# Two-layer hybrid backbone: large products as one float32 matmul in place of three float32r matmuls on high and low parts, and the MLP's tiles taken in groups of four

## The chip, the cores and the metric

The kernel runs on one core of a Trainium2 chip. The metric is the device time of one execution in microseconds, the median of several runs; lower is better. One profiled execution gives the trace from which all rows below are taken. The engines are named as the profile names them: PE (matrix multiplication; PEld is its weight load), DVE (vector), ACT (scalar, activations), POOL (general purpose) and SP, whose queue issues all DMAs of this kernel.

## The reference

Two layers over 1024 latent tokens and 256 context tokens of width 1024, everything in float32:

```
for i in range(DEPTH):                      # DEPTH = 2
    h  = modulate(x,  norm1_g, sh1, sc1)    # adaLN: rmsnorm(x, g) * (1 + scale) + shift
    (q, k, v), feat = project_tokens(h, w_in, ...)   # ONE input projection, 1024 -> 2480 columns
    attn = mla_attend(q, k, v)              # 8 heads, q/k of 96, v of 64; softmax over 1280 keys
    gdn  = gdn_mix(feat, ...)               # bidirectional gated delta rule, 4 heads of 128
    x = x + g1 * (concat([attn, gdn]) @ w_out)
    x = x + g2 * (square(relu(modulate(x, norm2_g, sh2, sc2) @ w_ff1)) @ w_ff2)   # D_FF = 4096
return rmsnorm(x, final_norm_g)
```

The context tokens go through the same weights, attend only to themselves, and are dropped after attention in the last layer. The modulation vectors are `silu(c) @ w_ada + b_ada`.

## The kernel before

Features lie with the 1024 channels on partitions, in 8 tiles (`KD` = 8), and the tokens along the free side in three blocks (`BLOCKS`): 256 context tokens, then twice 512 latent tokens. A product with a [128, 1024] weight tile is therefore 8 matmuls of 128 x 128 weights over 256 or 512 columns that accumulate in one bank of PSUM. Each layer has three stages.

Stage 1 (`stage1`): the norm, the input projection (`product`, 20 weight tiles of output columns), a short convolution on DVE (`conv_tile`, L442 to L450), the low-rank key, value and query projections (`kv_proj`, `q_proj`), and the chunk preparation of the delta rule (`Prep.decay`, with the product `dps` at L1421).

Stage 2 (`stage2`): attention in units of 256 queries of one head, 40 units in layer 0 and 32 in layer 1, and between them the steps of the delta rule (`delta`, its products are `g`). A unit has a `front` (scores `S` and `St`, their maximum, the exponential, the reciprocal of the sums) and a `back` (transposes `pt`, then the product with the values, `o`, at L916). The front of one unit is interleaved with the back of the unit before (`PATTERN`). The reciprocals go through DRAM (`rinv`, L902, then `rb`, L904) so that they lie along the queries; `ob` is the unit's result times `rb`.

Stage 3 (`stage3`): the output projection (`out_tile`, `ops`), the second norm, and the MLP: `ff1` makes one tile of 128 hidden columns for one block (`fps`, then relu and square), `ff2` multiplies a group of `FB` such tiles by the second weight (`f2ps`) and DVE adds the result to `x` at L1304. In layer 0, DVE also computes the modulation of later norms by multiply-and-sum in this stage (`ada_tile`, L272).

All large products are made in float32r: each operand is kept as a float32r high part and the remainder as a low part, and `mm3` issues high x high, high x low and low x high into the same bank. `wload` loads a weight tile and makes its parts: ACT copies the high part (L307), POOL subtracts to get the low part (L308). `norm_mod`, `lowrank`, `parts`, `ff1` and stage 3's load of `cat` do the same for the features. For attention, the low part of the values lies beside the high part in one 128-column weight, and the probabilities are split on the way out of PSUM: ACT makes `ph` (L927), DVE makes `pl` (L928). The small products of the delta rule, the transposes and the first modulation (`row`, L199) are plain float32 already.

Python code issues the instructions in program order; a scheduler of the tile framework then orders them on each engine by its own estimate of time. Each engine, and SP's queue of DMAs, runs its list in order.

Of the kernel before, what the change touches and what calls it, by code (L numbers as in the profile page):

```python
# [8 lines left out]
F32 = mybir.dt.float32  # L9
F32R = mybir.dt.float32r  # L10
BF16 = mybir.dt.bfloat16
AF = mybir.ActivationFunctionType
ALU = mybir.AluOpType
# [4 lines left out]
P = 128  # L18
# [16 lines left out]
W_BUFS = 3  # L35
# [38 lines left out]
def host_layout(inp):  # L74
# [16 lines left out]
    # tiles of output columns: q 4, k 4, v 4, misc, kv_a, q_a 2, z 4  # L91
# [4 lines left out]
    # the rotary columns: first halves of all heads, second halves of all heads  # L96
# [19 lines left out]
class K:  # L116
# [13 lines left out]
    # ---------------------------------------------------------------- set-up  # L130
# [35 lines left out]
    def start(self, mmp, pjp, tpp, stp):  # L166
        """Modulation of the first norm, the first norm, and the first two output tiles, as the features come."""
        nc, io, cst = self.nc, self.io, self.cst
        with ExitStack() as es:
# [12 lines left out]
            # features and weights are queued behind the modulation's weights  # L182
# [64 lines left out]
            for d in range(2):  # L247
                t = cst.tile([P, P], F32R, name=f"mlr{d}")
# [27 lines left out]
    def ada_sum(self, l, v, m):  # L276
        """Eight columns that came by way of Pool and ACT, from their halves and the bias."""
# [4 lines left out]
    def load_sc(self, sp):  # L282
        """silu(c) and silu(c_ctx) on all partitions."""
# [6 lines left out]
    def gain(self, l, j, vs):  # L290
        """(1 + scale) * gain of norm j."""
# [19 lines left out]
    def mm3(self, ps, lh, ll, rh, rl, start, stop, then=lambda i: None):  # L311
        mm = self.nc.tensor.matmul
        then(mm(ps, lhsT=lh, rhs=rh, start=start, stop=False))  # L313
        then(mm(ps, lhsT=lh, rhs=rl, start=False, stop=False))  # L314
        then(mm(ps, lhsT=ll, rhs=rh, start=False, stop=stop))  # L315
# [21 lines left out]
    def norm_mod(self, xs, rb, b, l, which, pool):  # L337
        """Modulated RMSNorm of block b (8 tiles [128, n]) into the high and low parts of h."""
# [478 lines left out]
    def attention(self, l, last, ap, psA, psO):  # L817
# [4 lines left out]
        def parts(hi, lo, src):  # L822
# [669 lines left out]
```

## Time and profile before

| | |
|---|---|
| time, median of 3 runs | 3947.9 us (3941.03 to 3948.28) |
| span of the profiled execution, first to last instruction | 3929.9 us |
| what lies around the span (median less span) | 18.0 us |
| PE busy | 3517.4 us (90%), 19001 matmul records |
| DVE, ACT, POOL busy | 2134.2 us (54%), 1459.3 us (37%), 1516.0 us (39%) |
| mean granted clock of PE | 0.937 of full speed |
| DMA | 372.52 MB, mean 95 GB/s |

"Busy" is the time during which at least one instruction of the engine is under way. Successive matmuls overlap in the array, so the duration of a single record is longer than the distance from its start to the next one's start; for a stream it is the distance that counts. "x12" in a row of the timeline means twelve records that follow one another. The granted clock is 1.00 at 2.4 GHz and 0.50 at 1.2 GHz; values between are averages over a stretch.

### The profile page before, as it was taken

The numbers are of one execution on the slowest core, as the hardware profiler recorded it, in microseconds if no ns is written. First come the engines' busy times: TensorE is split into PE (matmuls) and PEld (weight loads), VectorE is DVE, ScalarE is ACT, GpSimd is POOL, SyncE is SP. The second block draws the span as 40 slices with busy tenths as digits, with TensorE's granted clock in tenths as the row PEclk, the third lists the DMA queues.
The fourth block names the chain that finished last, engine by engine and source line by source line (L and its number), as shares of the span: only waits on it lengthen the run. The fifth ranks groups of instructions, "written<-read, shape, count | busy, mean of one in ns | idle before, by whom it ended". The sixth has DMA issues, their size and how long they took to land.

```text
span 3929.9 us, 52618 instructions
## 1 busy us (share of the span) xinstructions
PE 3517.4 (90%) x19001; PEld 2992.1 (76%) x19001; DVE 2134.2 (54%) x4080; ACT 1459.3 (37%) x3156; POOL 1516.0 (39%) x1358
## 2 busy tenths in 40 slices
PE   8789977887887898999999978888889899999998
PEld 4668766787776777888888757767788788888887
DVE  5157855565769995333333627776667533333334
ACT  4334355565633111121112524336666531222122
POOL 3124864433354232232223313675533352333232
PEclk8899987898998899999999979989899899999999
DMA  5343465535353352111111334454653511111111
GB/s 186 91 136 116 139 149 94 112 93 95 77 199 102 129 180 81 43 44 38 38 33 43 102 94 132 144 147 109 125 101 81 132 57 46 52 51 49 44 54 54
DMA packets 335892, 372.52 MB, mean 95 GB/s; under 512 B 126849, under 2 KB 226577, under 8 KB 333969
## 3 DMA queue, kind: packets, MB, share of 16 engines
q1 hardware_dynamic: 335632, 369.18, 34.3%
q8 instruction: 149, 2.44, 0.3%
q14 instruction: 111, 0.90, 0.1%
HBM read 280.65 MB, written 88.42 MB: 94 GB/s over the span
## 4 chain that ended last, share of the span: by engine, by line
PE 57%; DVE 13%; DMA 12%; issue 5%; ACT 4%; POOL 3%; SPq 1%; POOLq 0%; DVEq 0%; ACTq 0%
PE f2ps L313 6%; PE f2ps L314 6%; PE f2ps L315 6%; PE fps L314 6%; PE fps L315 6%; PE fps L313 6%; DVE adaj L272 3%; DMA raw<-kd 3%; PE g L984 3%; PE o L916 3%; PE pt L924 2%; DVE cacc L444 2%; DVE A L1427 2%; DMA rinv<-rinv 2%; DMA adaw<-w_adaT 1%
## 5 line engine op out<-in xcount | busy, mean ns | idle before, releaser
L308 POOL TENSOR_TENSOR wlo<-wraw,whi 128x1024 fp32r<-128x1024 f32 (+1 forms) x190 | 462.3, 2441 | 1217.8 <-ACT whi L307 1217.8
L1304 DVE SCALAR_TENSOR_TENSOR x<-f2ps,mod,x 128x512 f32<-128x512 f32 (+1 forms) x648 | 440.9, 689 | 353.3 <-PE f2ps L315 353.1
L307 ACT CAST whi<-wraw 128x1024 fp32r<-128x1024 f32 (+1 forms) x190 | 195.6, 1046 | 1008.0 <-PE f2ps L314 692.7
L313 PE MATMUL f2ps<-ah,whi 128*128 128x512 f32 (+1 forms) x1296 | 474.4, 371 | 31.4 <-DVE x L1304 27.2
L314 PE MATMUL f2ps<-al,whi 128*128 128x512 f32 (+1 forms) x1296 | 478.5, 370 | 0.8 <-DVE al L1293 0.8
L313 PE MATMUL fps<-hh,whi 128*128 128x512 f32 (+1 forms) x1288 | 471.3, 368 | 8.8 <-ACT hh L351 8.8
L315 PE MATMUL f2ps<-ah,wlo 128*128 128x512 f32 (+1 forms) x1296 | 477.4, 369 | 0.0
L314 PE MATMUL fps<-hl,whi 128*128 128x512 f32 (+1 forms) x1288 | 474.1, 368 | 0.0
L315 PE MATMUL fps<-hh,wlo 128*128 128x512 f32 (+1 forms) x1288 | 472.9, 368 | 0.0
L1293 DVE TENSOR_TENSOR al<-relu,ah 128x256 fp32r<-128x256 f32 (+1 forms) x161 | 111.5, 699 | 512.9 <-POOL relu L1292 512.9
L313 PE MATMUL mm<-hh,whi 128*128 128x512 f32 (+1 forms) x880 | 333.1, 380 | 35.0 <-ACT craw L430 22.1
L314 PE MATMUL mm<-hl,whi 128*128 128x512 f32 (+1 forms) x880 | 331.4, 377 | 3.6 <-DVE hl L352 2.1
L315 PE MATMUL mm<-hh,wlo 128*128 128x512 f32 (+1 forms) x880 | 327.6, 374 | 0.8 <-POOL wlo L308 0.8
L928 DVE TENSOR_TENSOR pl<-pt,ph 128x512 fp32r<-128x512 f32 x328 | 222.2, 686 | 194.7 <-ACT ph L927 182.1
L313 PEld LDWEIGHTS f2ps<-ah,whi 128*128 128x128 f32 x1296 | 248.2, 192 | 74.4 <-DVE x L1304 29.9
L313 PEld LDWEIGHTS fps<-hh,whi 128*128 128x128 f32 x1288 | 243.7, 190 | 49.1 <-ACT hh L351 9.1
L314 PEld LDWEIGHTS f2ps<-al,whi 128*128 128x128 f32 x1296 | 248.7, 192 | 40.7 <-DVE al L1293 1.0
L315 PEld LDWEIGHTS f2ps<-ah,wlo 128*128 128x128 f32 x1296 | 248.4, 192 | 40.1
L314 PEld LDWEIGHTS fps<-hl,whi 128*128 128x128 f32 x1288 | 244.0, 189 | 40.1 <-POOL hl L357 0.3
L315 PEld LDWEIGHTS fps<-hh,wlo 128*128 128x128 f32 x1288 | 243.9, 189 | 39.8
L924 PE MATMUL pt<-ctab,p 128*128 128x128 f32 x1312 | 219.9, 287 | 32.9 <-ACT p L896 12.7
L1292 POOL TENSOR_TENSOR relu<-relu 128x256 f32<-128x256 f32 (+1 forms) x161 | 159.5, 996 | 225.2 <-ACT ah L1291 209.7
(287 smaller groups left out, 7520.6 us busy)
## 6 DMA issues: line engine op xcount, KB each, us to landing
wraw<-w_ff SPq DMA_DIRECT2D x128, 512.0 KB
adaw<-w_adaT SPq DMA_DIRECT2D x160, 256.0 KB
wraw<-w_in SPq DMA_DIRECT2D x40, 512.0 KB
QK<-QK SPq DMA_DIRECT2D x72, 256.0 KB
A<-A SPq DMA_DIRECT2D x40, 256.0 KB
v<-vtd SPq DMA_DIRECT2D x40, 256.0 KB
kt<-ktd SPq DMA_DIRECT2D x40, 256.0 KB
kT<-kTd SPq DMA_DIRECT2D x36, 256.0 KB
```

What stands on the lines that cost most here:

```text
L272: nc.vector.tensor_tensor_reduce(out=j, in0=w, in1=self.sc_b[v][:, s], op0=ALU.mult, op1=ALU.add, scale=1.0, scalar=acc if i else self.bad ...
L307: nc.scalar.copy(hi[:, :n], raw[:, :n])
L308: nc.gpsimd.tensor_tensor(lo[:, :n], raw[:, :n], hi[:, :n].bitcast(F32), op=ALU.subtract)
L313: then(mm(ps, lhsT=lh, rhs=rh, start=start, stop=False))
L314: then(mm(ps, lhsT=lh, rhs=rl, start=False, stop=False))
L315: then(mm(ps, lhsT=ll, rhs=rh, start=False, stop=stop))
L916: nc.tensor.matmul(o, lhsT=v[:, k, :], rhs=x[:, j, :], start=k == 0 and i == 0, stop=k == nkt - 1 and i == 1)
L924: self.mark = nc.tensor.transpose(tp[:, j, i * P:(i + 1) * P], pp[i][:, (k0 + j) * P:(k0 + j + 1) * P], self.ident)
L928: nc.vector.tensor_tensor(pl, tp, ph.bitcast(F32), op=ALU.subtract)
L984: nc.tensor.matmul(ps[:, h, :], lhsT=lhs[:, h, :], rhs=rhs[:, h, :], start=True, stop=True)
L1292: nc.gpsimd.tensor_tensor(r[:, :n], r[:, :n], r[:, :n], op=ALU.mult)
L1304: nc.vector.scalar_tensor_tensor(xs, ps[:, :n], g2, xs, op0=ALU.mult, op1=ALU.add)
```

## The change

The high and low parts go away. Weights, features, keys, queries, values and probabilities are kept as float32, and each product is a single float32 matmul. With the parts go the instructions that made them: the ACT copies and POOL or DVE subtractions in `wload`, `norm_mod`, `lowrank`, `parts`, `Prep.decay`, `ff1` and the load of `cat`. The probabilities leave PSUM in one copy, alternately by ACT and DVE. The values are a 64-column weight, so the unit's result needs no addition of two halves, and DVE multiplies it by `rb` straight out of PSUM (before: ACT copied a half, DVE added, POOL multiplied). The squared relu is made by POOL alone. The memory that this frees goes into 10 weight tiles in flight (3 before), into 4 tiles `pt`, and into groups of four MLP tiles (`FB` = 4), which halves the number of `f2ps` groups that DVE adds to `x`; the modulation's columns are spread over the 8 groups accordingly.

```
-W_BUFS = 3
+W_BUFS = 10
...
-        hi = self.wp.tile([P, D], F32R, tag="whi", name="whi", bufs=self.wbufs)
-        lo = self.wp.tile([P, D], F32R, tag="wlo", name="wlo", bufs=self.wbufs)
         n = src.shape[-1]
-        raw = self.wp.tile([P, D], F32, tag="wraw", name="wraw", bufs=2)
-        nc.sync.dma_start(raw[:, :n], src)
-        with self.hp_():
-            nc.scalar.copy(hi[:, :n], raw[:, :n])
-            nc.gpsimd.tensor_tensor(lo[:, :n], raw[:, :n], hi[:, :n].bitcast(F32), op=ALU.subtract)
-        return hi, lo
+        w = self.wp.tile([P, D], F32, tag="w", name="w", bufs=self.wbufs)
+        self.nc.sync.dma_start(w[:, :n], src)
+        return w
...
-                self.mm3(ps[:, :n], w[0][:, s], w[1][:, s], *self.h[b][k], k == 0, k == KD - 1)
+                nc.tensor.matmul(ps[:, :n], lhsT=w[:, s], rhs=self.h[b][k], start=k == 0, stop=k == KD - 1)
...
-                self.mm3(s, qh[:, q], ql[:, q], t["kh"][:, c0:c1], t["kl"][:, c0:c1], True, True)
+                nc.tensor.matmul(s, lhsT=qq[:, q], rhs=kk[:, c0:c1], start=True, stop=True)
...
-            def pv(k0, ph, pl):
-                for i, x in enumerate((ph, pl)):
-                    for j in range(2):
-                        k = k0 + j
-                        nc.tensor.matmul(o, lhsT=v[:, k, :], rhs=x[:, j, :], start=k == 0 and i == 0,
-                                         stop=k == nkt - 1 and i == 1)
+            def pv(k0, pt):
+                for j in range(2):
+                    k = k0 + j
+                    nc.tensor.matmul(o[0:64], lhsT=v[:, k, :], rhs=pt[:, j, :], start=k == 0, stop=k == nkt - 1)
...
-                nc.scalar.copy(ph, tp)
-                nc.vector.tensor_tensor(pl, tp, ph.bitcast(F32), op=ALU.subtract)
-                wait.append((k0, ph, pl))
+                pt = ap.tile([P, 2, 256], F32, tag="pt", name="pt", bufs=4)
+                (nc.vector.tensor_copy if k0 % 4 else nc.scalar.copy)(pt, tp)
+                wait.append((k0, pt))
...
-            nc.scalar.copy(oh[0:64], o[64:128])
             ob = ap.tile([P, 256], F32, tag="ob", name="ob", bufs=2)
-            nc.vector.tensor_tensor(ob[0:64], o[0:64], oh[0:64], op=ALU.add)
-            nc.gpsimd.tensor_tensor(ob[0:64], ob[0:64], rb[0:64], op=ALU.mult)
+            nc.vector.tensor_tensor(ob[0:64], o[0:64], rb[0:64], op=ALU.mult)
...
-        FB = 2
+        FB = 4
...
                 nc.scalar.activation(r[:, :n], ps[:, :n], AF.Relu)
-                nc.scalar.activation(hi[:, c], r[:, :n], AF.Square)
-                nc.gpsimd.tensor_tensor(r[:, :n], r[:, :n], r[:, :n], op=ALU.mult)
-                nc.vector.tensor_tensor(lo[:, c], r[:, :n], hi[:, c].bitcast(F32), op=ALU.subtract)
-                yield hi, lo
+                nc.gpsimd.tensor_tensor(a[:, c], r[:, :n], r[:, :n], op=ALU.mult)
+                yield a
...
-            ps = self.pjp.tile([P, H_G, P], F32, tag="pj", name="dps")
-            for i in range(2):
-                nc.tensor.matmul(ps, lhsT=kk.mlr[d], rhs=gm[i], start=i == 0, stop=False)
+            ps = self.pjp.tile([P, H_G, P], F32, tag="pj", name="dps")
+            nc.tensor.matmul(ps, lhsT=kk.mlr[d], rhs=gm, start=True, stop=False)
```

On PE, in the MLP of layer 0, the second products of the first 512-token block stood in this order before (`ah` and `al` are the parts of the activations, `whi` and `wlo` those of the weight; the numbers tell tiles apart):

```order
L313 MATMUL f2ps_12546<-ah_12246,whi_12374 128x512 [waits DVE_49]
L314 MATMUL f2ps_12546<-al_12247,whi_12374 128x512
L315 MATMUL f2ps_12546<-ah_12246,wlo_12375 128x512
L313 MATMUL f2ps_12546<-ah_12278,whi_12380 128x512
L314 MATMUL f2ps_12546<-al_12279,whi_12380 128x512
L315 MATMUL f2ps_12546<-ah_12278,wlo_12381 128x512
L313 MATMUL f2ps_12554<-ah_12246,whi_12374 128x512 [waits DVE_49]
```

A bank is filled by 2 tiles of the hidden layer with 3 matmuls each, and the next bank begins with the seventh instruction.

At the same place on PE, with the change:

```order
L1239 MATMUL f2ps_9078<-a_8822,w_8926 128x512 [waits DVE_49,Pool_49]
L1239 MATMUL f2ps_9078<-a_8835,w_8928 128x512 [waits Pool_49]
L1239 MATMUL f2ps_9078<-a_8848,w_8930 128x512 [waits Pool_49]
L1239 MATMUL f2ps_9078<-a_8861,w_8932 128x512 [waits Pool_49]
L1239 MATMUL f2ps_9084<-a_8822,w_8926 128x512 [waits DVE_49]
L1239 MATMUL f2ps_9084<-a_8835,w_8928 128x512
```

A bank is now filled by 4 tiles with one matmul each; PE waits for POOL, which writes `a`, where it waited for ACT and DVE.

On DVE, in stage 2 of layer 0, near the first product with the values, the order before was (`p` and `mx` are scores taken out of their bank and their maxima, `U` a block of the delta rule's inverses):

```order
L928 TENSOR_TENSOR pl<-pt,ph 128x512 [waits Activation_49]
L878 TENSOR_SCALAR p,mx<-S 128x512 [waits PE_49]
L878 TENSOR_SCALAR p,mx<-St 128x256 [waits PE_49]
L878 TENSOR_SCALAR p,mx<-St 128x256
L895 TENSOR_REDUCE mn<-mx 128x1 [waits DVE_49]
L1016 COPY U_4383<-B_4365 32x4x32 [waits DMAHW1_49]
L1016 COPY U_4385<-B_4365 32x4x32
L940 TENSOR_TENSOR ob<-o_4364,oh 64x256 [waits Activation_49]
```

DVE's part of `ob` waited for ACT alone; the product with `rb` stood on POOL.

On DVE, in stage 2 of layer 0 with the change, where a full unit's `ob` is followed by that of a unit of context tokens:

```order
L889 TENSOR_TENSOR ob<-o_3012,rb 64x256 [waits DMAHW1_49,DMAHW0_49,PE_49]
L1078 TENSOR_TENSOR oss<-oss,alq_1723 128x4 [waits Activation_49]
L1079 TENSOR_SCALAR oss<-oss 128x4 [waits DVE_49]
L833 TENSOR_SCALAR p,mx<-S 128x512 [waits PE_49]
L1082 TENSOR_TENSOR orr<-orr,alq 128x4 [waits Pool_49]
L833 TENSOR_SCALAR p,mx<-S 128x512 [waits PE_49]
L850 TENSOR_REDUCE mn<-mx 128x1 [waits DVE_49]
L833 TENSOR_SCALAR p,mx<-S 128x512 [waits PE_49]
L889 TENSOR_TENSOR ob<-o_3012,rb 64x256 [waits DMAHW2_49,DMAHW0_49,PE_49]
```

DVE itself now waits for the DMA that brings `rb`, and the scores of the next unit stand behind it in its list.

## Rows read from the trace of the kernel before

**Rows 1.** The page: PE's busy time, share of the span, matmul records.

```profile
PE 3517.4 (90%) x19001; PEld 2992.1 (76%) x19001; DVE 2134.2 (54%) x4080; ACT 1459.3 (37%) x3156; POOL 1516.0 (39%) x1358
```

**Rows 2.** Busy time of each engine by stage: start:end, length, engines, granted clock, DMA.

```profile
core 0: us, PE busy (x) PEld busy (x) DVE busy (x) ACT busy (x) POOL busy (x), PEclk, DMA share, GB/s
...
46.00:512.00 466.00, 406.29 (x2106) 341.69 (x2107) 278.06 (x315) 180.27 (x456) 219.45 (x173) 0.91 0.39 114
512.00:1098.00 586.00, 462.36 (x3175) 417.18 (x3174) 351.36 (x1022) 347.63 (x843) 246.37 (x324) 0.87 0.50 102
1098.00:1241.00 143.00, 118.78 (x606) 100.13 (x606) 119.14 (x205) 38.62 (x76) 77.62 (x48) 0.94 0.53 179
1241.00:1500.00 259.00, 226.24 (x1106) 193.61 (x1107) 236.20 (x461) 60.33 (x98) 78.50 (x51) 0.90 0.45 144
1500.00:2170.00 670.00, 670.00 (x3500) 577.91 (x3500) 248.92 (x392) 135.09 (x212) 178.67 (x121) 1.00 0.13 40
2170.00:2612.00 442.00, 374.60 (x1824) 305.68 (x1823) 266.96 (x307) 168.50 (x411) 207.13 (x157) 0.92 0.40 119
2612.00:3117.00 505.00, 427.97 (x3010) 385.45 (x3008) 330.95 (x936) 322.34 (x756) 231.69 (x308) 0.90 0.50 107
3117.00:3210.00 93.00, 91.59 (x403) 75.80 (x402) 21.47 (x30) 25.30 (x36) 38.86 (x25) 0.97 0.35 121
3210.00:3930.00 720.00, 705.98 (x3192) 587.06 (x3192) 268.84 (x395) 168.46 (x247) 231.57 (x145) 0.99 0.16 49
```

**Rows 3.** PE's costliest groups by shape: shape, count, busy, mean ns, idle before.

```profile
L313 PE MATMUL fps<-hh,whi 128*128 128x512 f32 x1016 | 393.9, 390 | 1.6 <-ACT hh L351 1.6
L313 PE MATMUL f2ps<-ah,whi 128*128 128x512 f32 x1008 | 390.2, 393 | 2.9 <-DVE x L1304 2.9
L313 PE MATMUL mm<-hh,whi 128*128 128x512 f32 x640 | 260.5, 408 | 24.4 <-ACT craw L430 20.5 <-ACT zc L557 3.5 <-DVE kp L598 0.4
L916 PE MATMUL o<-pl,v 128*128 128x256 f32 x656 | 158.8, 326 | 25.7 <-DVE pl L928 25.5
L313 PE MATMUL f2ps<-ah,whi 128*128 128x256 f32 x288 | 84.3, 295 | 28.5 <-DVE x L1304 24.3 <-ACT relu L1290 4.2
```

**Rows 4.** Timeline of PE: float32r streams of 512 and of 256 columns; start, length.

```profile
1499.81 0.39 PE L313 MATMUL f2ps<-ah,whi 128*128 128x512 f32 x1
...
1509.78 0.39 PE L315 MATMUL f2ps<-ah,wlo 128*128 128x512 f32 x1
...
512.61 0.28 PE L313 MATMUL St<-kh,qh 96*128 96x256 f32 x1
...
513.32 0.28 PE L313 MATMUL St<-kh,qh 96*128 96x256 f32 x1
```

**Rows 5.** Plain float32 matmuls: two tiles' records, two streams of the timeline, one window.

```profile
L199 PE MATMUL row<-wa,scT x64: 591/592/1061, 6.5 to 39.6; 128*2 128x512 f32 x64
...
27.90 7.14 PE L199 MATMUL row<-wa,scT 128*2 128x512 f32 x16
...
27.90:35.00 7.10, 7.10 (x17) 1.19 (x16) 0.16 (x1) 1.95 (x3) 3.04 (x2) 1.00 1.02 410
...
1008.21 1.50 PE L984 MATMUL g<-S,kT 128*128 128x128 f32 x12
...
L984 PE MATMUL g<-S,kT x144: 270/275/422, 578.9 to 1012.9; 128*128 128x128 f32 x144
```

**Rows 6.** Who waited for whom: stage 2 and the MLP of layer 0; us, times, longest.

```profile
PE o L916 <- ACT ph L927: 37.4, 12, 11.0
...
ACT kh L832 <- DMA raw<-kd: 83.5, 18, 10.1
...
PE f2ps L313 <- DVE x L1304: 27.0, 7, 9.2
```

**Rows 7.** Timeline of SP and POOL: one reciprocal on its way through DRAM.

```profile
824.41 0.54 SPq L902 DMA_DIRECT2D rinv<-rinv  x1
832.57 0.46 SPq L904 DMA_DIRECT2D rb<-rinv  x1
...
836.86 0.71 POOL L941 TENSOR_TENSOR ob<-ob,rb 64x256 f32<-64x256 f32 x1 [3.64 <-DMA rb<-rinv]
```

More of the change, by code (lines that the diff above doesn't have):

```diff
@@ L646, in gates @@
         nc.vector.reciprocal(be, be)
-        ghi = sm.tile(sh, F32R, tag="ghi", name="ghi")
-        nc.scalar.copy(ghi, g)
-        self.ghi, self.glo = ghi.bitcast(F32), new("glo")
-        nc.vector.tensor_tensor(self.glo, g, self.ghi, op=ALU.subtract)
+        self.g = g
         ps = stp.tile([P, 512], F32, tag="st", name="cum")
         tabs = [self.ctab[:, c:c + P] for c in (C_M0, C_M1, C_ONE)]
-        tabs[2:2] = [m.bitcast(F32) for m in self.mlr]
+        tabs[2:2] = self.mlr
         for i, d in enumerate((0, 1, 0, 1, 0, 1)):
@@ L733, in kv_proj @@
                 s = slice(m * P, (m + 1) * P)
-                self.mm3(ps[:, :n], wh[:, s], wl[:, s], xh[:, :n], xl[:, :n], True, True)
+                nc.tensor.matmul(ps[:, :n], lhsT=w[:, s], rhs=x, start=True, stop=True)
                 t = self.staged(sp, ps[:, :n], n)
@@ L739, in kv_proj @@
                 ps = mmp.tile([P, 512], F32, tag="pj", name="vps")
-                self.mm3(ps, xh[:, o:o + P], xl[:, o:o + P], wh[:, 512:], wl[:, 512:], True, True)
+                nc.tensor.matmul(ps, lhsT=x[:, o:o + P], rhs=w[:, 512:], start=True, stop=True)
                 e = self.staged(sp, ps, 512)
@@ L759, in qmm @@
                 for k in range(2):
-                    self.mm3(ps[:, :n], wk[k][0][:, s], wk[k][1][:, s], x[k][0][:, :n], x[k][1][:, :n], k == 0, k == 1)
+                    nc.tensor.matmul(ps[:, :n], lhsT=wk[k][:, s], rhs=x[k], start=k == 0, stop=k == 1)
                 return ps
@@ L861, in front @@
                 load(h)
[L862 to L863 removed]
+            kk, v = cur[h]
+            qq = cur[h, b]
             nk = NCTX if b == 0 else NT
@@ L1166, in stage3 @@
         self.side(l + 1)
-        self.open_wh(blocks, W_BUFS + last)
+        self.open_wh(blocks)
         es = ExitStack()
-        ec, et = ExitStack(), ExitStack()
-        cp = ec.enter_context(self.pool(f"s3c_{l}", side=self.msd))
+        et = ExitStack()
         tp = et.enter_context(self.pool(f"s3a_{l}", side=self.osd))
@@ L1205, in out_tile @@
                 s = slice(k * P, (k + 1) * P)
-                self.mm3(ps[:, :n], w[0][:, s], w[1][:, s], *cat[k, b], j == 0, j == KD - 1)
+                nc.tensor.matmul(ps[:, :n], lhsT=w[:, s], rhs=cat[k, b], start=j == 0, stop=j == KD - 1)
             g1 = self.mod[l][1 if b == 0 else 0][:, 16 + m:17 + m]
@@ L1287, in ff1 @@
                     s = slice(k * P, (k + 1) * P)
-                    self.mm3(ps[:, :n], w[0][:, s], w[1][:, s], *(t[:, c] for t in self.h[b][k]), k == 0, k == KD - 1)
-                r = mp.tile([P, 512], F32, tag="relu", name="relu", bufs=2)
+                    nc.tensor.matmul(ps[:, :n], lhsT=w[:, s], rhs=self.h[b][k][:, c], start=k == 0, stop=k == KD - 1)
+                r = mp.tile([P, 512], F32, tag="relu", name="relu", bufs=3)
                 nc.scalar.activation(r[:, :n], ps[:, :n], AF.Relu)
-                nc.scalar.activation(hi[:, c], r[:, :n], AF.Square)
-                nc.gpsimd.tensor_tensor(r[:, :n], r[:, :n], r[:, :n], op=ALU.mult)
-                nc.vector.tensor_tensor(lo[:, c], r[:, :n], hi[:, c].bitcast(F32), op=ALU.subtract)
-                yield hi, lo
+                nc.gpsimd.tensor_tensor(a[:, c], r[:, :n], r[:, :n], op=ALU.mult)
+                yield a
         def ff2(w, act, b, c, m):
@@ L1300, in ff2 @@
             for i, a in enumerate(act):
-                self.mm3(ps[:, :n], w[i][0][:, s], w[i][1][:, s], *(t[:, c] for t in a), i == 0, i == FB - 1)
+                nc.tensor.matmul(ps[:, :n], lhsT=w[i][:, s], rhs=a[:, c], start=i == 0, stop=i == FB - 1)
             g2 = self.mod[l][1 if b == 0 else 0][:, 40 + m:41 + m]
@@ L1318, in stage3 @@
             w2 = [self.wload(io["w_ff2"][l, f]) for f in fs]
-            for a in ada[8 * fi:8 * fi + 8] if fi == 0 else ada[4 * fi + 4:4 * fi + 8]:
+            for a in ada[8 * fi:8 * fi + 8]:
                 self.ada_tile(*a, adp, 512)
```

95 lines of the change are left out of this document (23 added, 72 removed).

## Prediction

> **What bounds the kernel now.** I read the page first. PE is busy for 90% of the span [rows 1], and no other engine passes 54%. An average hides stages, so the next view is the busy time by stage [rows 2]. The reader should see three kinds. From 1500 to 2170 us and from 3210 to the end, the MLP, PE is busy without a gap or nearly so, at a granted clock of 1.00 and 0.99: here whatever PE gets to do is added to the time. From 46 to 512 and from 2170 to 2612 (stage 1) and in stage 2 (512 to 1098, 2612 to 3117) PE is busy 79 to 87% and the clock stands at 0.87 to 0.92, that is, PE spends part of these stages at 1.2 GHz after it has waited; they are bound partly by PE and partly by chains through the others. From 1241 to 1500 it is DVE that is full (236 of 259 us, the modulation and the additions to x), and PE waits for it [rows 2, 6]. The waits in stage 2 show what those chains are: PE waits for ph, which ACT makes, and ACT itself sat 83.5 us before it could split keys that had not landed [rows 6].
>
> **What a product costs, before and after.** The durations of single records overlap, so I take distances between starts. Before: from 1499.81 to 1509.78 us there are 44 steps of a 512-column float32r matmul, 0.2266 us each; a product of three is 0.680 us. With 256 columns it is six steps in 0.71 us, 0.118 each, 0.355 a product [rows 4].
>
> The kernel already has plain float32 matmuls, and they decide the case. The modulation at the start calls 8 x 4 = 32 matmuls of 512 columns (loops of 8 and 4 in `start`), and the trace has 64 records of them: a float32 matmul runs as two records. Sixteen of these records take 7.14 us with the last one's 0.592 us included, so one is (7.14 - 0.59) / 15 = 0.4367 us, at a granted clock of 1.00 [rows 5]; 0.4367 us is 1048 cycles of 2.4 GHz, two for each column. A float32 product of 512 columns is then 2 x 0.437 = 0.873 us, where three float32r matmuls were 0.680: **+0.193 us**, 28% more. Those weights are only 2 columns wide; that full weights don't change it is seen in the delta rule, where 12 records of 128 x 128 weights over 128 columns take 1.50 us, (1.50 - 0.27) / 11 = 0.112 us each [rows 5], again two cycles a column (0.27 us is the end of the last one). For 256 columns I interpolate by columns between 0.112 and 0.437: 0.220 a record, 0.440 a product, +0.085 us. The bounds are 0.224 (a record no dearer than with 128 columns) and 0.873; nearest to the straight line is the two-cycles rule, so I keep it.
>
> **The change on PE, part by part.** [Rows 3] give the counts. Products of 512 columns: 1016 fps, 1008 f2ps and 640 mm, and by the code's loops 256 S, 256 ops and 84 in the low-rank projections: 3260 x 0.193 = +630 us. Products of 256 columns: 288 f2ps and, by the loops, 740 more: 1028 x 0.085 = +88 us. The product with the values had two float32r matmuls of 256 columns for 128 keys (ph and pl, 0.237 us) and gets one float32 of 0.440: 656 x 0.203 = +133 us. Narrower weights don't help, since the time goes by the columns that stream through. The 40 dps products go from 0.453 to 0.873: +17 us. Together **+868 us of PE time**. By stage, with the loops' counts: stage 1 +93 and +86, stage 2 +100 and +95, output projection +30 and +25, MLP +242 (layer 0) and +197 (layer 1).
>
> **What is taken from the others, and what that returns.** POOL loses the 190 low parts of weights, ACT as many copies; in stage 2 the two passes over each block of probabilities become one, shared by ACT and DVE; the additions to x on DVE are halved by FB = 4. None of these engines bounds a stage but DVE from 1241 to 1500, so the gain is only in the gaps of PE:
> - MLP, layer 0, 1241 to 1500: 33 us of PE's time are gaps. DVE's work falls while PE's grows, so DVE stops setting the pace. I take back 22; the first norm's chain remains.
> - Stage 1: gaps of 60 and 67 us. They come from the convolution and from projections whose results ACT stages; 40% goes under the longer products: 24 and 27.
> - Stage 2: gaps of 124 and 77 us. ACT no longer stands before unlanded keys, and the way from pt to the product is one copy, not two. But the keys' DMA still has to land, and then PE waits itself. Half: 62 and 38.
> - Output projection, layer 0: 8 of 24 us. Rest of the MLP: nothing, there are no gaps.
>
> Returned: 181 us. Bounds: 0, and for stages 1 and 2 their whole +374 with about 30 elsewhere. The squared relu on POOL, the copy of pt on DVE and the deeper prefetch are costed at nothing: an ff1 product lasts 8 x 0.873 = 7 us, and one POOL or DVE instruction lies beside it; if it didn't, the last one of each group would add its length, about 1 us for 16 groups.
>
> **Sum.** 868 - 181 = +687 us on the span of 3930, so 4617, and with the 18 us around the span 4635 us, against a median of 3947.9 of the runs shown.
>
> **The rivals.** (1) *Nothing is returned*: the gaps are latencies of in-order lists that a slower PE only pushes on. For it speaks that PE's waits in stage 2 have many causes. 3948 + 868 = 4816; less than 100 returned is 4716 or more. (2) *Stages 1 and 2 swallow their share*: their gaps (328 us together) and the slow clock are worth nearly the 374 us added; then 868 - 374 - 30 = +464, 4412. For it: in layer 0's stage 2 the clock stands at 0.87, and a PE with fewer gaps would run more of it at 2.4 GHz [rows 2]; against it: DMA latencies stay. (3) *DVE is held up by rb*: the multiplication by rb moves from POOL to DVE. One reciprocal left at 824.41, its return was issued at 832.57, and ob began at 836.86 after waiting for it [rows 7], 12.5 us in all; POOL could wait, but behind DVE's ob stand the scores of the next unit, and PE's banks behind these. It costs where the order of DVE reaches ob within 12.5 us of the reciprocal, which the short context units and the last unit of each head come near to: 16 heads of the two layers at 6 to 12 us, +100 to +190 on my forecast, 4735 to 4825. (4) *On the other side, one record a product*: if the two records of row were an oddity of 2-column weights and a float32 product of full width were one record of 0.437 us, products would get cheaper: 3260 x (0.437 - 0.680) = -792, 1028 x (0.220 - 0.355) = -139, the values -11, together -942 and about 3005 us at best. It decides as soon as a product is below 0.680 us. Against it: the delta rule's full-width matmuls have two records for each call too (9 steps x 2 directions x 4 heads are 72 calls of g<-S,kT in layer 0, and the trace has 144 records [rows 5]).
> The Trainium skill speaks for this rival: Perfetto Trace Analysis, Engine Utilization, halves PE's output rate for FP32_LOW_HIGH, which as an estimate for a whole product would be 427 ns for 512 columns. By that rule the change would gain; the trace agrees only if it is applied to each of the two records, and the skill's FP8 and Floating Point Precision, TensorE Precision Notes, says four passes, an estimate of 853 ns, beside 873 here.
>
> **How the numbers follow.** Between 100 and 260 us returned, 0.62: 4556 to 4716, around 4635. Rival 1, 0.14; rival 2 (more than 260 returned, 4412 to 4556), 0.16; rival 3, 0.05; rival 4, 0.03. The range, 4470 to 4780, leaves out the far ends of rivals 1 to 3 and rival 4. Against no change, 0.2% (8 us) is what a measurement can tell here: faster 0.03, same 0.01, slower 0.96.
>
> **What would show it.** Right: about 14700 matmul records on PE (19001, less a third of the products' 12860); 0.873 us for two records of fps or f2ps; the last MLP near 915 us instead of 720, layer 0's from 929 to about 1150; a granted clock higher in stage 2; DVE no longer full at the start of layer 0's MLP. Wrong: a product below 0.68 us; a DVE that waits long for rb in stage 2 (rival 3); gaps of PE in stage 2 as large as before (rival 1) or a stage 2 no longer than 586 and 505 us (rival 2).

## The result, and the profile after

The changed kernel takes **4518.7 us** (median of four runs, 4515.9 to 4522.0) against 3948.0 for the kernel before (3941.0 to 3948.3): a ratio of 1.1441, 95% interval 1.1422 to 1.1460. It is slower by 571 us; the forecast was slower by 687, and the time lies inside the range. The profiled spans are 4520.2 and 3929.9 us, 590 apart.

The first row of the page, which answers to [rows 1]:

```profile
PE 4276.8 (95%) x14745; PEld 2334.6 (52%) x14745; DVE 1505.0 (33%) x3303; ACT 982.4 (22%) x2383; POOL 762.1 (17%) x886
```

14745 records of PE where 14700 were forecast: every large product has two records now, not three. Every other engine has lost work, and PE has gained 759 us of busy time.

Busy time by stage, which answers to [rows 2] (the same stages in the same order; each begins with the first record of its first tile):

```profile
core 0: us, PE busy (x) PEld busy (x) DVE busy (x) ACT busy (x) POOL busy (x), PEclk, DMA share, GB/s
44.00:584.00 540.00, 482.06 (x1567) 271.25 (x1567) 224.30 (x300) 155.18 (x417) 168.71 (x200) 0.94 0.37 107
584.00:1171.00 587.00, 545.75 (x2966) 357.74 (x2966) 281.94 (x893) 257.51 (x654) 104.67 (x133) 0.97 0.46 102
1171.00:1362.00 191.00, 152.65 (x415) 80.52 (x415) 157.91 (x368) 30.20 (x66) 47.03 (x33) 0.89 0.60 186
1362.00:1640.00 278.00, 262.45 (x732) 142.23 (x733) 98.73 (x221) 20.34 (x40) 24.54 (x25) 0.96 0.29 91
1640.00:2479.00 839.00, 839.00 (x2350) 445.53 (x2349) 111.84 (x176) 52.66 (x101) 67.32 (x79) 1.00 0.10 33
2479.00:2966.00 487.00, 437.40 (x1360) 231.12 (x1359) 206.16 (x285) 136.84 (x364) 150.20 (x171) 0.94 0.38 108
2966.00:3511.00 545.00, 526.73 (x2820) 336.86 (x2818) 268.88 (x818) 241.47 (x589) 106.12 (x146) 0.97 0.51 98
3511.00:3626.00 115.00, 113.41 (x277) 51.31 (x277) 17.77 (x26) 12.39 (x20) 13.65 (x11) 1.00 0.32 96
3626.00:4520.00 894.00, 883.89 (x2174) 409.60 (x2172) 125.67 (x191) 63.05 (x111) 77.42 (x76) 1.00 0.11 37
```

Against [rows 2], with the forecast in brackets: stage 1 of layer 0 +74 (+69), stage 2 **+1 (+38)**, output projection **+48 (+22)**, MLP of layer 0 +188 (+220); stage 1 of layer 1 +45 (+59), stage 2 +40 (+57), output projection +22 (+25), the last MLP +174 (+197). Two rows want an explanation. Stage 2 of layer 0 has 83 us more of PE's work and is 1 us longer: PE's idle time fell from 124 to 41 us and its clock rose from 0.87 to 0.97. The output projection of layer 0 lost more than its products: PE stands idle for 38 of 191 us, and DVE is busy for 158.

The timeline of PE gives the new price (start, length, records), as [rows 4, 5] gave the old one:

```profile
35.29 3.60 PE L198 MATMUL row<-wa,scT 128*2 128x512 f32 x8 [1.59 <-DMA wa<-w_ada]
...
2003.79 8.58 PE L1239 MATMUL f2ps<-a,w 128*128 128x256 f32 x39
...
2479.97 7.89 PE L1239 MATMUL f2ps<-a,w 128*128 128x512 f32 x18
```

Eighteen records of f2ps are (7.89 - 0.59) / 17 = 0.429 us each (the last record's own length is taken off), so a float32 product of 512 columns takes 0.859 us, not 0.873; with 256 columns it is (8.58 - 0.38) / 38 = 0.216 a record and 0.432 a product, not 0.440.

### The profile page after: what moved, and what is told of

It is laid out like the page before. It is cut to its first block, busy times and chain, and to the rows that moved or that the text cites. A ratio compares the mean times of both kernels' runs of the same rounds, so it can differ in the third digit from the quotient of the medians.

```text
span 4520.2 us, 40823 instructions
## 1 busy us (share of the span) xinstructions
PE 4276.8 (95%) x14745; PEld 2334.6 (52%) x14745; DVE 1505.0 (33%) x3303; ACT 982.4 (22%) x2383; POOL 762.1 (17%) x886
## 4 chain that ended last, share of the span: by engine, by line
PE 80%; DMA 7%; POOL 4%; DVE 4%; issue 3%; SPq 1%; ACT 1%; POOLq 0%; DVEq 0%; ACTq 0%
PE f2ps L1239 22%; PE fps L1228 21%; PE mm L395 9%; PE o L870 7%; PE S L827 5%; PE g L932 4%; PE pt L877 4%; PE ops L1147 2%; DVE adaj L271 2%; POOL both L1400 2%; POOL btmp L1397 2%; DMA rinv<-rinv 1%; DMA adaw<-w_adaT 1%; PE St L827 1%; DMA qd<-stg 1%
## 5 line engine op out<-in xcount | busy, mean ns | idle before, releaser
L1239 PE MATMUL f2ps<-a,w 128*128 128x512 f32 (+1 forms) x2624 | 997.3, 542 | 15.5 <-DVE x L1242 15.5
L1228 PE MATMUL fps<-h,w 128*128 128x512 f32 (+1 forms) x2576 | 996.4, 549 | 1.6 <-ACT h L335 1.6
L1239 PEld LDWEIGHTS f2ps<-a,w 128*128 128x128 f32 x2624 | 500.7, 191 | 505.2 <-issue 471.6
L1242 DVE SCALAR_TENSOR_TENSOR x<-f2ps,mod,x 128x512 f32<-128x512 f32 (+1 forms) x328 | 224.4, 685 | 1584.0 <-PE f2ps L1239 1583.9
L1228 PEld LDWEIGHTS fps<-h,w 128*128 128x128 f32 x2576 | 491.3, 191 | 500.9 <-issue 484.6
L395 PE MATMUL mm<-h,w 128*128 128x512 f32 (+1 forms) x1760 | 689.5, 546 | 24.0 <-DVE kp L576 13.3
L395 PEld LDWEIGHTS mm<-h,w 128*128 128x128 f32 x1760 | 338.0, 195 | 330.6 <-issue 287.7
L870 PE MATMUL o<-pt,v 128*64 128x256 f32 x1312 | 345.7, 393 | 10.5 <-DVE ob L889 10.5
L827 PE MATMUL S<-k,q 96*128 96x512 f32 x512 | 271.7, 617 | 10.5 <-DVE p L833 8.2
L1147 PE MATMUL ops<-cat,w 128*128 128x512 f32 (+1 forms) x640 | 257.9, 565 | 12.8 <-DVE x L1149 10.4
```

The source lines that it names most:

```text
L395: nc.tensor.matmul(ps[:, :n], lhsT=w[:, s], rhs=self.h[b][k], start=k == 0, stop=k == KD - 1)
L827: nc.tensor.matmul(s, lhsT=qq[:, q], rhs=kk[:, c0:c1], start=True, stop=True)
L870: nc.tensor.matmul(o[0:64], lhsT=v[:, k, :], rhs=pt[:, j, :], start=k == 0, stop=k == nkt - 1)
L1147: nc.tensor.matmul(ps[:, :n], lhsT=w[:, s], rhs=cat[k, b], start=j == 0, stop=j == KD - 1)
L1228: nc.tensor.matmul(ps[:, :n], lhsT=w[:, s], rhs=self.h[b][k][:, c], start=k == 0, stop=k == KD - 1)
L1239: nc.tensor.matmul(ps[:, :n], lhsT=w[i][:, s], rhs=a[:, c], start=i == 0, stop=i == FB - 1)
```

## The experiments

The later runs were on other chips, where the kernel before took 3968 to 3972 us. The table names for each the kernel from which it departs, its median, its ratio to the kernel before with the 95% interval, and from its trace the length of stage 2, output projection and MLP of layer 0, then of stage 2 and MLP of layer 1. Here stage 2 begins with the first S. A trace is of one execution: that of scores_f32 lies 18 us below the median of its runs, that of split_pool 12 us above.

| kernel | departs from | median us | ratio to before | stage 2 | out | MLP | stage 2 | MLP |
|---|---|---|---|---|---|---|---|---|
| before | | 3948.0 | 1 | 576.5 | 142.9 | 940.5 | 504.6 | 719.7 |
| after | | 4518.7 | 1.1441 [1.1422, 1.1460] | 581.4 | 191.5 | 1126.9 | 531.8 | 895.7 |
| after_again | after | 4517.6 | 1.1368 [1.1349, 1.1387] | 586.0 | 191.0 | 1124.2 | 532.4 | 895.4 |
| fb2 | after | 4490.2 | 1.1308 [1.1287, 1.1328] | 581.5 | 150.3 | 1130.0 | 531.8 | 899.5 |
| ob_pool | after | 4505.6 | 1.1347 [1.1326, 1.1367] | 565.0 | 193.2 | 1128.9 | 526.9 | 895.2 |
| ada_held | after | 4465.3 | 1.1248 [1.1228, 1.1268] | 586.2 | 152.6 | 1106.8 | 530.9 | 895.4 |
| combo | after | 4444.6 | 1.1187 [1.1168, 1.1205] | 562.4 | 155.7 | 1106.8 | 528.6 | 895.0 |
| scores_f32 | before | 3898.1 | 0.9835 [0.9812, 0.9858] | 535.9 | 145.7 | 936.0 | 494.4 | 720.0 |
| pv_f32 | before | 4049.9 | 1.0212 [1.0194, 1.0230] | 625.8 | 146.9 | 942.5 | 563.0 | 720.8 |
| mlp_f32 | before | 4339.5 | 1.0941 [1.0921, 1.0961] | 602.0 | 138.7 | 1132.7 | 510.6 | 899.5 |
| split_pool | before | 3932.9 | 0.9908 [0.9888, 0.9928] | 573.5 | 140.9 | 938.9 | 521.6 | 720.7 |
| scores_pv | before | 4006.4 | 1.0079 [1.0059, 1.0099] | 613.5 | 138.8 | 934.4 | 550.9 | 722.9 |

**The kernel after, again.** No edit.

> The kernel after, unchanged, on the chip of the next runs, since the kernel before took 3968 us on the chips of the last runs and 3948 on the first. If only what waits for transfers differs between chips, this kernel, which waits less, stays within 10 us of 4519, and the spans of the earlier runs can be compared with its 4520 directly; if the whole chip is slower, 4540 or more.

4517.6 us beside 4518.7 on the first chip, while the kernel before took 24 us more here (3972.3). So the kernels that depart from after are compared with 4518 us directly, and those that depart from before by their ratios. The stages of before that were left alone show where its own time moves: in mlp_f32, whose stage 2 has the code of before, that stage of layer 0 took 602.0 us, not 576.5. Where a stage 2 of the later runs is set beside that of before, some 25 us of layer 0's can therefore be the chip's.

**price: what a product costs by itself.** Streams of products into one bank, with nothing between:

```
def stream(name, count, m, n, r=False):
    a, b = (wr, xr) if r else (w, x)
    ...
    for i in range(count):
        c = (i % 8) * P
        nc.tensor.matmul(t[0:m, 0:n], lhsT=a[:, c:c + m], rhs=b[:, 0:n], start=i == 0, stop=i == count - 1)
```

> Measures the disputed price by itself; it leaves out the whole computation of the reference and keeps only streams of products, each into one bank, the first two streams beside a steady traffic of weight loads, the rest without. In the kernel after, a record of row (2-column weights) had 0.4367 us and a record of fps 0.430 us. Theory 'two records, two cycles a column, whatever the weights': every float32 stream has two records a product; full_a, thin_b, fulld and thind all have 0.427 to 0.431 us a record, half_b and val_b 0.214 to 0.218; 0.4367 was something of the start of the kernel. Rival 'narrow weights are dearer': thind and thin_b at 0.436 or more, the others 0.430. Rival 'traffic': fulld and thind above 0.434, thin_b and full_a below 0.431. float32r: real_a 0.226 and realhalf_a 0.118 a product as in the kernel before; if these streams show 0.213 and 0.107 instead, what made them dearer was something around them in the kernel. One record a product (my rival 4) is already out by the count of records of the kernel after; here it would be 32 records in full_a.

Windows of that kernel from the start of a stream to that of the next, in this order: fulld (20 products), thind (20), full_a (32), thin_b (32), real_a (96 float32r, 512 columns), half_b (32), realhalf_a (96 float32r, 256 columns); the counts take in a record or two of the neighbours:

```profile
21.16:38.42 17.26, 17.26 (x42) 7.41 (x40) 0.16 (x1) 0.00 (x0) 0.00 (x0) 1.00 1.03 410
38.42:55.68 17.26, 17.26 (x42) 3.32 (x41) 0.16 (x1) 0.00 (x0) 0.00 (x0) 1.00 1.03 409
90.11:117.67 27.56, 27.56 (x65) 11.97 (x63) 0.16 (x1) 0.00 (x0) 0.00 (x0) 1.00 0.00 1
117.67:145.23 27.56, 27.56 (x65) 5.36 (x64) 0.16 (x1) 0.00 (x0) 0.00 (x0) 1.00 0.00 0
145.23:167.14 21.91, 21.91 (x97) 18.13 (x97) 0.15 (x1) 0.00 (x0) 0.00 (x0) 1.00 0.00 1
167.14:180.77 13.63, 13.63 (x66) 11.99 (x64) 0.16 (x1) 0.00 (x0) 0.00 (x0) 1.00 0.01 1
180.77:192.56 11.79, 11.79 (x99) 11.63 (x97) 0.16 (x1) 0.00 (x0) 0.00 (x0) 1.00 0.00 0
```

Each window also holds the change to the next stream, so the pace is read from the streams' own starts and lengths:

```profile
21.16 17.33 PE L144 MATMUL fulld<-x,w 128*128 128x512 f32 x40
38.42 17.33 PE L144 MATMUL thind<-x,w 128*2 128x512 f32 x40
...
90.11 27.63 PE L144 MATMUL full_a<-x,w 128*128 128x512 f32 x64
117.67 27.63 PE L144 MATMUL thin_b<-x,w 128*2 128x512 f32 x64
145.23 22.07 PE L144 MATMUL real_a<-xr,wr 128*128 128x512 f32 x96
167.14 13.97 PE L144 MATMUL half_b<-x,w 128*128 128x256 f32 x64
180.77 11.86 PE L144 MATMUL realhalf_a<-xr,wr 128*128 128x256 f32 x96
192.56 14.03 PE L144 MATMUL val_b<-x,w 128*64 128x256 f32 x64
```

Without its last record's own length (0.59 us), a stream of 64 is (27.63 - 0.59) / 63 = 0.429 us a record with full and with 2-column weights, and one of 40 is (17.33 - 0.59) / 39 = 0.429 under 410 GB/s of loads. So neither the width of the weights nor the traffic made the 0.4367 that I read from row of the kernel before [rows 5] (the expectation says the kernel after, by mistake); the same tile's last 8 records in the kernel after are (3.60 - 0.59) / 7 = 0.430 as well. The trace of before shows what made it: the stream of 16 is two runs of 8 records, from 27.90 and from 31.45 us, each 3.60 us long, with one step of 0.54 us between them, at the change to the next weight tile. Three float32r matmuls are 3 x (22.07 - 0.39) / 95 = 0.685 us, one float32 product 0.858: +0.174 with 512 columns. With 256 columns a record takes (13.97 - 0.38) / 63 = 0.216 us, and nearly as much with 64-column weights (val_b, 0.217): a product is 0.431 us, three float32r matmuls are 3 x (11.86 - 0.28) / 95 = 0.366.

**mlp_f32: the MLP alone.** In the kernel before, h of the second norm, the squared relu and the MLP's weights become float32, in groups of two as before:

```diff
-                    self.mm3(ps[:, :n], w[0][:, s], w[1][:, s], *(t[:, c] for t in self.h[b][k]), k == 0, k == KD - 1)
+                    nc.tensor.matmul(ps[:, :n], lhsT=w[:, s], rhs=self.h[b][k][:, c], start=k == 0, stop=k == KD - 1)
...
-                self.mm3(ps[:, :n], w[i][0][:, s], w[i][1][:, s], *(t[:, c] for t in a), i == 0, i == FB - 1)
+                nc.tensor.matmul(ps[:, :n], lhsT=w[i][:, s], rhs=a[:, c], start=i == 0, stop=i == FB - 1)
```

> The kernel before, with only the MLP in float32 (its norm, ff1, squared relu, ff2; groups of two tiles, weights in the same buffers as before). PE gets 2048 products of 512 columns and their share of 256 at 0.859 against 0.680: +224 us in layer 0 and +183 in layer 1, +407. Theory 'no gaps to hide it in but the start of layer 0': +360 to +390, 4308 to 4338, the last MLP at 890 to 900 us. Rival 'the whole change's other parts paid for part of the MLP': more than +400, 4350 or more. If it falls below +340, products in the MLP cost less than their columns.

A ratio of 1.0941 is +371 us on 3948. The two MLPs are 192 and 180 us longer: together 372, the whole difference, and close to what they gained in after (186 and 176 by the same bounds). The median lies 1.5 us above the first theory's 4308 to 4338, which was worked out from 3948 us for before. The MLP accounts for two thirds of the change's cost, and its price is nearly the columns': 180 of 183 us in layer 1, and 192 of 224 in layer 0, where before had 36 us of gaps.

**scores_f32 and pv_f32: the two halves of attention alone.** In the kernel before, first only the scores:

```diff
-                t[nm] = (ap2 if h % 2 else ap1).tile([DQK, NT], F32R, tag=nm, name=nm)
-            parts(t["kh"], t["kl"], self.kd[h])
+            t = {"k": (ap2 if h % 2 else ap1).tile([DQK, NT], F32, tag="k", name="k")}
+            nc.sync.dma_start(t["k"], self.kd[h])
...
-                self.mm3(s, qh[:, q], ql[:, q], t["kh"][:, c0:c1], t["kl"][:, c0:c1], True, True)
+                nc.tensor.matmul(s, lhsT=qq[:, q], rhs=t["k"][:, c0:c1], start=True, stop=True)
```

> The kernel before, with only the scores of the latent attention as single float32 products: keys and queries are loaded as they are, so ACT and DVE or POOL no longer split them. PE gets 256 products of 512 columns at +0.179 us (0.859 by the pitch in the kernel after) and about 150 of 256 columns at +0.08: +58 us. Theory 'stage 2 of layer 0 hides behind its gaps because ACT no longer stands before unlanded keys': most of it is swallowed, 3938 to 3975, and the 83.5 us of ACT waiting for raw are gone. Rival 'the gaps stay and PE pays': 3995 to 4010.

and then only the product with the values, with one copy of pt and rb on DVE as in after:

```diff
-                nc.scalar.copy(ph, tp)
-                nc.vector.tensor_tensor(pl, tp, ph.bitcast(F32), op=ALU.subtract)
+                (nc.vector.tensor_copy if k0 % 4 else nc.scalar.copy)(pt, tp)
...
-            nc.vector.tensor_tensor(ob[0:64], o[0:64], oh[0:64], op=ALU.add)
-            nc.gpsimd.tensor_tensor(ob[0:64], ob[0:64], rb[0:64], op=ALU.mult)
+            nc.vector.tensor_tensor(ob[0:64], o[0:64], rb[0:64], op=ALU.mult)
```

> The kernel before, with only the product with the values as single float32 products: one copy of pt, shared by ACT and DVE, in place of a copy and a subtraction, and the multiplication by rb on DVE. PE gets 656 x (0.432 - 0.237) = +128 us. Theory 'the way from pt to the product bound stage 2, and half of the added columns goes under its gaps': 3990 to 4040. Rival 'PE pays all': 4070 to 4080. Other rival 'this is the part that swallows': below 3985, so that the kernel with this alone costs less than a third of its columns.

The scores alone make the kernel **faster** than before, by 1.65%: better than either theory. Stage 2 of both layers in scores_f32, by windows; PE's wait for ph in its layer 0 (us, times, longest); and the same two windows of pv_f32:

```profile
519.30:1055.20 535.90, 459.24 (x2960) 368.13 (x2960) 347.95 (x1007) 321.57 (x791) 189.10 (x257) 0.93 0.53 105
...
2572.90:3067.30 494.40, 434.69 (x2813) 350.29 (x2812) 331.80 (x934) 305.92 (x722) 186.64 (x265) 0.93 0.54 108
```

```profile
PE o L914 <- ACT ph L925: 15.8, 6, 8.7
```

```profile
521.10:1146.90 625.80, 543.28 (x3164) 393.61 (x3164) 290.38 (x902) 289.61 (x716) 198.48 (x250) 0.92 0.48 92
...
2676.00:3239.00 563.00, 509.03 (x3004) 363.31 (x3002) 277.62 (x837) 272.76 (x647) 194.68 (x257) 0.94 0.52 97
```

In scores_f32 PE is busy for 459 us, as before (461 by the same bounds), though its columns cost some 29 us more: more of them ran at 2.4 GHz, the mean clock being 0.93 and not 0.88. PE's gaps fell from 116 to 77 us; ACT no longer waits for keys, and PE waits 16 us for ph, not 37 [rows 6]. On the chip of scores_f32 the code of before stood worse than in its own trace (mlp_f32: 138 us of gaps, 42.8 for ph), so the comparison may understate the gain. In pv_f32 PE's busy time grows by 82 us in each layer, where the columns account for about 64 (the rest is not explained), and the stages by 49 and 58 beside before, 24 and 52 beside mlp_f32. A ratio of 1.0212 is +84 us for 128 us of columns: within the first theory (3990 to 4040, with the 20 us by which this chip's runs of before are longer).

**split_pool: is it ACT's wait?** All products stay float32r; only the copy to the high part of the keys goes to POOL:

```diff
-                nc.scalar.copy(hi[:, c:e], raw)
+                (nc.gpsimd.tensor_copy if p == DQK and m == NT else nc.scalar.copy)(hi[:, c:e], raw)
```

> The kernel before, where the high part of the keys is taken by POOL instead of ACT; all products stay as they were. The scores alone in float32 made stage 2 of layer 0 41 us and of layer 1 10 us shorter though PE got more columns. Theory 'it was ACT standing in order before keys that had not landed (83.5 us), with ph queued behind it': with that wait on POOL, which PE hardly waits for, most of the gain comes without any float32 product: 1.0 to 1.7% faster than before. Rival 'it was the work of splitting as such, or three products in place of one': less than 0.5% faster, or slower, since POOL now takes over a microsecond a piece.

Waits of stage 2, layer 0 (us, times, longest):

```profile
POOL kh L832 <- DMA raw<-kd: 63.6, 16, 9.6
...
ACT v L832 <- DMA raw<-vd: 50.4, 6, 15.1
```

PE's wait for ph in stage 2 of split_pool, layer 0 and then layer 1:

```profile
PE o L916 <- ACT ph L927: 19.9, 9, 7.5
```

```profile
PE o L916 <- ACT ph L927: 72.9, 11, 18.1
```

It is faster by 0.92% (0.72 to 1.12), between the theory's 1.0 to 1.7% and the rival's 0.5%, and nearer the theory. So over half of what the scores returned comes back without any float32 product, from taking one copy off ACT. That ACT's place in order before the keys is what cost is argued, not shown: POOL stands there now, ACT stands 50.4 us before the values (8.7 in before), and the copies' own time (21 of 0.55 us) left ACT as well. The trace doesn't show where the time comes back: PE waits less for ph in layer 0 (37 before) and more in layer 1 (42 before), and its gaps in stage 2 are 114 and 100 us, where before has 116 and 77. The rest of what the scores returned (0.7%) is the work of splitting or the three products, which this run doesn't separate.

**scores_pv: do the two halves add?** Both edits above in one kernel.

> The kernel before, with all of the latent attention of stage 2 in float32 (scores and the product with the values) and nothing else changed. Alone, the scores gave 0.9835 of before and the values 1.0212. Theory 'they return different gaps, and add': 1.000 to 1.008, stage 2 of layer 0 at 575 to 590 us and of layer 1 at 530 to 553. Rival 'both live on the same gaps': the second finds them gone, 1.012 or more.

1.0079, where the two ratios multiply to 1.0044: at the upper edge of the first theory by the ratio, and stage 2 of layer 0 longer than it said (613.5 us, not 575 to 590), that of layer 1 within its 530 to 553 (550.9). They nearly add. But the same attention takes 581 to 586 and 532 us in the kernel after, some 30 and 19 less. What else in after shortens stage 2 by that wasn't tried.

**fb2: groups of two again.** In the kernel after:

```diff
-        FB = 4
+        FB = 2
...
-            for a in ada[8 * fi:8 * fi + 8]:
+            for a in ada[8 * fi:8 * fi + 8] if fi == 0 else ada[4 * fi + 4:4 * fi + 8]:
```

> The kernel after with groups of two MLP tiles as before the change, so twice the additions to x: 192 more on DVE in layer 0 and some 128 in layer 1, at 0.66 us each. Theory 'PE's columns set the MLP': DVE is far from full behind the first stretch, so the MLP of layer 1 stays at 894 us within 5, layer 0 loses at most 10, and the whole is within 12 us of 4519. Rival 'the groups of four gave back part': layer 0's start is bound by DVE again, 30 us or more there, and 4550 or more in all.

Neither: 28 us *less* than after. The MLPs behave as the first theory says (+3 and +4 us), but the output projection of layer 0 is 41 us shorter, which no theory had. The edit also spreads the modulation columns over twice as many groups, so that DVE has 80 of their pieces in that stage and not 160, and that is what counts, as the next run shows.

**ada_held: the modulation behind the norm.** In the kernel after, DVE takes the MLP's modulation columns only behind its last operation of the second norm (`held`):

```diff
+        held = self.last_norm
...
-                self.ada_tile(*a, adp, 512)
+                with self.tc.issue_after(held.ins):
+                    self.ada_tile(*a, adp, 512)
```

> The kernel after, where DVE may take the 80 modulation columns that are issued within the MLP of layer 0 only behind the second norm. The output projection of layer 0 grew by 48 us where its products account for 25 or less; DVE was busy for 158 of 191 us there with 160 pieces of the modulation, where the kernel before had 80. Theory 'the modulation came ahead of the norm and pushed it': 15 to 30 us less, 4489 to 4504, and the stage at 165 to 175 us. Rival 'it is the late transfer of rb and the chain of the norm': the pieces move, the stage stays within 5 us of 191, and the whole within 6 us of 4519. If the pieces crowd the first groups of the MLP instead, the MLP of layer 0 grows by as much as the stage before it loses.

DVE's groups in the output projection of layer 0 of after (1171 to 1362 us): line, operation, count | busy, mean ns | idle before.

```profile
L271 DVE CUSTOM_DVE_ANT_0 adaj<-adaw,scr,vec 128x512 bf16<-128x512 f32 x80 | 71.9, 914 | 10.8 <-DMA adaw<-w_adaT 10.7
L271 DVE CUSTOM_DVE_ANT_0 adaj<-adaw,scr,mod 128x512 bf16<-128x512 f32 x80 | 70.2, 893 | 0.0
L1149 DVE SCALAR_TENSOR_TENSOR x<-ops,mod,x 128x512 f32<-128x512 f32 (+1 forms) x24 | 15.4, 651 | 0.0
...
L889 DVE TENSOR_TENSOR ob<-o,rb 64x256 f32<-64x256 f32 x1 | 0.4, 416 | 26.3 <-DMA rb<-rinv 26.3
```

and who made PE wait there:

```profile
PE st L312 <- DVE nacc L1312: 10.5, 1, 10.5
PE ops L1147 <- DVE x L1149: 10.4, 3, 7.4
PE st L312 <- DVE h L334: 9.2, 1, 9.2
PE rb L320 <- POOL rs L317: 5.8, 1, 5.8
```

The same two views of ada_held's output projection, and the window of its MLP of layer 0:

```profile
L271 DVE CUSTOM_DVE_ANT_0 adaj<-adaw,scr,mod 128x512 bf16<-128x512 f32 x40 | 43.9, 1097 | 2.5 <-DMA adaw<-w_adaT 1.2
L271 DVE CUSTOM_DVE_ANT_0 adaj<-adaw,scr,vec 128x512 bf16<-128x512 f32 x40 | 39.0, 974 | 12.1 <-DMA adaw<-w_adaT 11.0
...
L889 DVE TENSOR_TENSOR ob<-o,rb 64x256 f32<-64x256 f32 x1 | 0.4, 417 | 24.9 <-DMA rb<-rinv 24.9
```

```profile
PE ops L1147 <- DVE x L1149: 5.4, 1, 5.4
...
PE st L312 <- DVE nacc L1314: 1.4, 1, 1.4
```

```profile
1327.60:2434.40 1106.80, 1105.51 (x3121) 588.85 (x3119) 286.49 (x573) 82.55 (x152) 92.44 (x104) 1.00 0.19 59
```

In after, 160 pieces of the modulation (142 us) stood among DVE's additions to x, its sums nacc and the norm's h, and PE waited for each of these. With 80 pieces the stage is 39 us shorter, and the other 80 cost nothing within the MLP, which is itself 20 us shorter, at 1105.5 of 1106.8 us busy. The transfer of rb is as late as before (24.9 us) and costs nothing seen here. The gain, 52 us, is more than the 15 to 30 that I expected: the stage fell below its 165 to 175 us, and I had not counted the MLP's start.

**ob_pool: rb off DVE.** In the kernel after:

```diff
-            nc.vector.tensor_tensor(ob[0:64], o[0:64], rb[0:64], op=ALU.mult)
+            nc.vector.tensor_copy(ob[0:64], o[0:64])
+            nc.gpsimd.tensor_tensor(ob[0:64], ob[0:64], rb[0:64], op=ALU.mult)
```

> The kernel after, where DVE only copies o out of its bank and POOL multiplies by rb, so DVE no longer waits for rb (38 us in stage 2 of the two layers and 26.3 us at the start of layer 0's output projection, by the waits of the kernel after). Theory 'those waits lie beside PE's work': the waits vanish, stage 2 stays within 5 us, the output projection of layer 0 starts its additions earlier but is held by the modulation on DVE all the same: 4510 to 4520. Rival 'DVE is held up by rb' (my rival 3): 25 to 50 us less, 4470 to 4495.

DVE's waits for rb in stage 2 and the output projection of after (589 to 1362 us), those in its stage 2 alone, and POOL's in stage 2 of ob_pool:

```profile
DVE ob L889 <- DMA rb<-rinv: 57.7, 7, 26.3
```

```profile
DVE ob L889 <- DMA rb<-rinv: 31.4, 6, 11.8
```

```profile
POOL ob L890 <- DMA rb<-rinv: 56.7, 8, 15.8
```

The wait moves to POOL and is longer there, and 13 us come back (4518.7 to 4505.6): 16 and 5 us in the two stages 2, less 2 to 3 us in the output projections. That lies between the two theories: the stall is real, and worth about a fifth of its length.

**combo.** Both edits: `issue_after` for the modulation, and rb on POOL.

> The kernel after with both: the modulation columns of the MLP held behind the second norm, and POOL multiplying by rb. Theory 'the two places are apart, the gains add' (54 us of the one, 13 of the other by the medians against 4519): 4445 to 4460. Rival 'both take away the same late start of the output projection': no better than the first alone, 4462 to 4470.

4444.6 us, 73 less than after_again on the same chip; the gains add (52 and 12 to 13, and some 8 more). This is the best kernel found with all products in float32; scores_f32, with only the scores, is the best of all, 1.65% below the kernel before.

## Why the prediction was right, and where its terms were off

The cause holds: PE bounds the kernel, and a float32 product costs more of PE's time than three float32r ones. price shows it with nothing around (0.858 against 0.685 us), mlp_f32 in the stage that has nearly no gaps. Rival 4, one record a product, is out by the 64 records for 32 products. The Trainium skill's halving for FP32_LOW_HIGH (Perfetto Trace Analysis, Engine Utilization) fits each record by itself: two cycles of 2.4 GHz a column would be an estimate of 427 ns, and the trace has 429.

Rival 1 is out too: PE's idle time in stage 2 fell by two thirds or more. Rival 2 came true in layer 0's stage 2 and in no other stage. Yet the time itself, 4519, lies in the band that I gave to rival 2 (4412 to 4556, 0.16) and not in my central one: 80 of the 116 us between 4635 and 4519 come from the price of a product and from the time around the span, and what was returned, 217 us, lies within my 100 to 260.

The 116 us come from three terms.
- **What a product costs.** 0.859 for 0.873 us, and 0.432 for 0.440 with 256 columns: the PE term is 3260 x 0.179 + 1028 x 0.077 + 656 x 0.195 + 16 = 807 us, not 868. I had taken 0.4367 us from one stream of row, which holds a stop; price and f2ps say 0.429. This is 61 us of the miss, on terms for products that are otherwise as counted.
- **What is returned.** 807 - 590 = 217 us, not 181, and in other places than I said. The large errors are two, of opposite sign, so that the sum is nearer than its parts, and that much is luck; the other stages are each within 15 us of what they were said to give back, at the measured price.
  - *Stage 2 of layer 0* gave back all but 1 of some 94 us (my 100 at the measured price), where I gave back 62. The step that was too low is "But the keys' DMA still has to land, and then PE waits itself": PE waits for no keys of the attention there, neither in after nor in scores_f32. scores_f32 and split_pool make it likely that ACT, standing in order before the keys, held up work that PE needed. But scores_pv, with the same attention, is 30 us longer in this stage than after, so about that much came back through something else in the change, and which part of it stays open. The rise of the clock from 0.87 to 0.97, which I gave only to rival 2, goes with the smaller gaps.
  - *The output projection of layer 0* lost 20 us beyond its products (28 at the measured price), where I gave it back 8. "DVE's work falls while PE's grows, so DVE stops setting the pace" was right for DVE from 1362 to 1640 us (99 of 278 busy) but not for the stage ahead: groups of four brought twice the modulation there. ada_held shows it: 39 us in this stage and 20 in the MLP.
- **Around the span.** I added 18 us, the median of before less its span. In the later runs time and span of a run are 2 us apart (3969.2 and 3967.4 for one of before), so those 18 us were most likely a profiled execution shorter than the others: 16 us too much, and in after the profiled execution was 3 us above the median.

Rival 3's mechanism was there, DVE waiting for rb 57.7 us from 589 to 1362 us, but at 13 us and not 100 to 190: of my 6 to 12 us a head, PE's other work hid most.

## What to carry to other kernels

When products get dearer, price the columns on the engine that streams them, from two or more streams of the trace, and then look at each stage's gaps for *which engine stands in order before a transfer*: moving one such copy to another engine gave back 0.9% here, and converting only the scores, whose keys were waited for, gave 1.65%, where converting all cost 14%. A change of a loop's group size also moves whatever rides on that loop; list what else is issued per group, and look for it in the stages before. Where a wait is seen on an engine, its price is found by moving the wait, and may be a fifth of its length.

## What the runs showed of the hardware that was not expected

- A float32r matmul is not one column a cycle: in price it takes 0.228 us for 512 columns, 548 cycles of 2.4 GHz (0.2266 in [rows 4]), while a record of a float32 product takes 0.429, 1030 cycles for the same columns, almost exactly two each. With 256 columns a float32r matmul takes 0.122 us, more than half of 0.228; the weight loads are busy there for 11.63 of 11.79 us, so they may set that pace (argued only).
- The width of the weights (2 or 128 columns) and 410 GB/s of loads beside the stream left a float32 record's pace with 512 columns at 0.429 us.
- The kernel before took 20 to 24 us more on the chips of the later runs, the kernel after 1 us less. The one that waits more for transfers is the one that differs; that the transfers are the cause wasn't tested.
